# A decoder trunk on one core: high weights against both activation halves in one 512-column matmul

## The chip, the cores and the metric

One core of one Trainium2 chip runs the whole program. The metric is device time in microseconds (us). The core's engines are TensorE (PE; its loads of the standing operand are listed as PEld), VectorE (DVE), ScalarE (ACT), GpSimd (POOL) and SyncE (SP), which issues most DMA transfers. SBUF is the working memory; TensorE writes its results to PSUM, in tiles that VectorE and ScalarE read.

## The reference

Two layers of a decoder on 256 tokens of 2048 channels, in float32. A layer normalises x, multiplies it by one wide matrix, runs four branches on slices of the result, gates and projects each branch, adds the four, projects once more and adds to x.

```python
h = rms_norm(x, g_pre[l])
(s5_u, s5_z, ml_q, ml_k, ml_v, ml_o, ml_z, ml_i, ml_f,
 da_q, da_k, da_v, da_z, xa_q, xa_z, gate_pre) = split_cols(h @ w_in[l], IN_SPLITS)
y_s5 = s5_mixer(s5_u, ...) * silu(s5_z)        # diagonal state space, then a GLU: y * sigmoid(y @ w_glu + b)
y_ml = mlstm_mixer(ml_q, ml_k, ...) * silu(ml_z)   # ml_q, ml_k go through a 4-tap causal convolution first
y_da = diff_attention(da_q, da_k, da_v, ...) * silu(da_z)
y_xa = memory_attention(xa_q, rms_norm(mem, g_mem[l]), xa_w_kv[l]) * silu(xa_z)
merged = sum(sigmoid(gate_pre[b]) * (y_b @ w_branch[l, b]) for b in the four branches)
x = x + rms_norm(merged @ w_out[l], g_post[l])
```

Each 1024-wide slice (s5_u, ml_q and so on) and both halves of xa_w_kv (K and V) are matrix products of depth 2048.

## The kernel before

**Split operands.** Every weight matrix and every activation is held as two float32r tiles: a rounded high half (wh, hh) and the remainder as a low half (wl, hl). A product is three matmuls: high x high, high x low, low x high, added up in PSUM (`mm3`, L354 to L358). hh and hl hold the normalised x, mh and ml the normalised memory, both transposed: channels on the 128 partitions, 256 tokens along the row.

**Units.** All weights come as one stream of 944 units in a fixed order (`plan`, `stream`). A unit is 512 KB, 128 partitions x 1024 values: two depth blocks of 128 by 512 output columns. SP loads it into `raw` (4 buffers); ScalarE copies it to `wh` (L303), VectorE writes `raw - wh` to `wl` (L206). Each has LA + 1 = 4 buffers, and `ahead` issues loads and splits of up to LA = 3 units beyond the one in use.

**Two kinds of group.** `tok_group` keeps activations standing in TensorE and streams 512 weight columns: the result has tokens on the partitions. `chan_group` keeps a 128 x 128 block of weights standing and streams the 256 tokens: the result has channels on the partitions. A unit holds 8 such blocks, 24 matmuls of 256 columns in this form, 12 of 512 columns in the other. A group runs over the whole depth (8 units; 4 in the GLU and in the branch projections) and fills two accumulator tiles `acc` of 128 x 512; there are four. `chan_group` serves K of the memory attention, s5_u, ml_q, ml_k, xa_q, xa_z, s5_z and the GLU; everything else is `tok_group`.

**Other work.** Branches, norms and the emptying of accumulators are Python generators. After each unit `used` calls `bg_step`, which lets each live generator issue its next piece; `evac` puts the pieces that empty a group's accumulators on that list. Each engine runs what it was given in the order of issue, so this list sets where a piece stands between the splits. `u_evac` writes s5_u to DRAM for the S5 branch (`s5_gen`), `conv_gen` is the convolution, `phase` a gate and a branch projection; `t2` is a pool of six scratch tiles, `ps` are PSUM tiles for small products.

**Order of a layer.** V, K, s5_u, the differential attention's projections, ml_v, ml_o, ml_z, ml_q, ml_k, the phase of the differential attention, xa_q, xa_z, the mLSTM's phase, s5_z, the memory attention's phase, the GLU, the S5 phase, the output projection. In layer 0, by the profile, K runs from 58.7 to 108.7 us, s5_u to 154.8, ml_q and ml_k from 493.7 to 587.6, xa_q and xa_z from 733.5 to 832.4, s5_z from 982.9 to 1029.4.

Of the kernel before, what the change touches and what calls it, by code (L numbers as in the profile page):

```python
# [8 lines left out]
F32 = mybir.dt.float32  # L9
# [81 lines left out]

def in_groups():
    g = []
    for c0, n in ((S5U, 2), (DAQ, 2), (DAK, 2), (DAV, 2), (DAZ, 2), (MLV, 2), (MLO, 2), (MLZ, 2), (MLQ, 2),
                  (MLK, 2), (XAQ, 2), (XAZ, 2), (S5Z, 2), (GATE, 16)):
        for i in range(n):
            g.append(c0 + 512 * i)
    return g
# [3 lines left out]
GIDX = {c: i for i, c in enumerate(GROUPS)}  # L102


def layout(inp):
    a = {k: np.asarray(v) for k, v in inp.items()}
    out = {}
# [5 lines left out]
    out["w_kv"] = tile_w(a["xa_w_kv"])  # L113
# [40 lines left out]
INS = ("x", "mem", "w_in", "w_if", "w_kv", "w_br", "w_glu", "w_out", "cols", "s5_b", "s5_c", "lqk", "g_post", "consts")  # L154
# [3 lines left out]
def body(tc, x, mem, w_in, w_if, w_kv, w_br, w_glu, w_out, cols, s5_b, s5_c, lqk, g_post, consts, out,  # L158
# [4 lines left out]
    with ExitStack() as ctx:  # L163
# [81 lines left out]
        for l in range(depth):  # L245
            pl = {}
            for g in (2, 3, 0, 1):
                pl["kv", g] = add_units(w_kv[l, g], 8)

            def win(c0, l=l, pl=pl):  # L250
                pl["in", c0] = add_units(w_in[l, GIDX[c0]], 8)

            for c in (S5U, DAQ, DAK):
# [4 lines left out]
            for c in (MLV, MLO, MLZ, MLQ, MLK):  # L258
                win(c)
                win(c + 512)  # L260

            def phase(b, l=l, pl=pl):
# [5 lines left out]
            for c in (XAQ, XAZ):  # L268
                win(c)
                win(c + 512)  # L270
            phase(1)
            win(S5Z)
            win(S5Z + 512)
# [147 lines left out]


# [38 lines left out]
        def norm_T(src, cl, gname, dst_h, dst_l):  # L461
# [8 lines left out]
            yield from scaled_T(src, cl, gname, dst_h, dst_l)  # L470

        def scaled_T(src, cl, gname, dst_h, dst_l):

            s, _ = COLS[gname]
            held = {}

            def st_T(j):
                p = ps()
                for i in range(2):
                    for t in range(2):  # L480
                        d = 2 * j + i
                        tr(p[:, i * 256 + t * 128:i * 256 + t * 128 + 128], src[t][:, d * 128:d * 128 + 128])
                held[j] = p

            def st_h(j):
                for i in range(2):
                    d = 2 * j + i
                    act(dst_h[d // 8][:, d % 8], held[j][:, i * 256:i * 256 + 256], AF.Identity, scale=cl[:, s + d:s + d + 1])

            def st_l(j):  # L490
                for i in range(2):
                    d = 2 * j + i
                    stt(dst_l[d // 8][:, d % 8], held[j][:, i * 256:i * 256 + 256], cl[:, s + d:s + d + 1],
                        dst_h[d // 8][:, d % 8], M_, S_)

            yield from ticks(8, 1, [(0, st_T), (1, st_h), (1, st_l)])

        def bank(hs):
            return lambda kb: hs[kb // 8][:, kb % 8]
# [17 lines left out]
        def mem_T(l, cl):  # L517
# [670 lines left out]
        mt, mh, mlo, mgen = mem_T(0, cl)  # L1188
# [28 lines left out]
        for l in range(depth):  # L1217
            pl = plan[l]
            last = l == depth - 1
            hh = [bigr("hh"), bigr("hh")]  # L1220
            hlo = [bigr("hl"), bigr("hl")]
            mhb, mlb = bank(mh), bank(mlo)
            xg = norm_T(x_t, cl, "g_pre", hh, hlo)
# [4 lines left out]
            for g in range(2):  # L1228
                o = tok_group(pl["kv", 2 + g], 8, mhb, mlb)
                evac(*[lambda: None] * 5,  # L1230
# [5 lines left out]
            for g in range(2):  # L1236
                o = chan_group(pl["kv", g], 8, mhb, mlb)
                evac(lambda o=o, g=g: [tt(blk2(kT8[:, (2 * g + i) * 512:(2 * g + i) * 512 + 512]), blk2(o[i]),
                                          mrb.unsqueeze(1).to_broadcast([128, 2, 256]), M_) for i in range(2)],
                     lambda g=g, vm=vm, kT8=kT8: g == 1 and [  # L1240
                         nc.gpsimd.dma_start(out=kdr, in_=kT8),
                         nc.gpsimd.dma_start(out=vdr, in_=vm.rearrange("p t d -> p (t d)"))])
            bg_finish(ng)
            hb, lb = bank(hh), bank(hlo)
# [96 lines left out]
            def conv_gen(o, dst, off, g):  # L1341
                tmps = {}

# [3 lines left out]
                def src(m):  # L1347
                    return o[m // 2][:, (m % 2) * 256:(m % 2) * 256 + 256]

                def c_a(i):  # L1350
                    tmps[i] = t2.tile([128, 2, 256], F32, name="cv", tag="t2")
                    for k in range(2):
                        m = 2 * i + k
                        blk = off + 4 * g + m
                        act(tmps[i][:, k], src(m), AF.Identity, scale=wc(3, blk), bias=pcol(cl, "conv_b", blk))

                def c_b(*js):
                    def f(i):
                        for j in js:
                            for k in range(2):  # L1360
                                m = 2 * i + k
                                stt(tmps[i][:, k, 3 - j:256], src(m)[:, 0:253 + j], wc(j, off + 4 * g + m),
                                    tmps[i][:, k, 3 - j:256], M_, A_)
                    return f

                def c_c(i):
                    act(dst[:, 4 * g + 2 * i:4 * g + 2 * i + 2], tmps[i], AF.Silu)

                yield from ticks((0, 3), 1, [(0, c_a), (1, c_b(0, 1)), (2, c_b(2)), (3, c_c)])

            s5b["rate"] = 0.5
            for c0, dst, off in ((MLQ, cq, 0), (MLK, ck, 8)):
                for g in range(2):
                    o = chan_group(pl["in", c0 + 512 * g], 8, hb, lb)
                    bg_add(conv_gen(o, dst, off, g))
# [41 lines left out]
            for c0, dst, fn in ((XAQ, xq, AF.Copy), (XAZ, xz, AF.Silu)):  # L1417
                for g in range(2):
                    o = chan_group(pl["in", c0 + 512 * g], 8, hb, lb)
                    evac(lambda o=o, g=g, dst=dst, fn=fn: [act(dst[:, 4 * g + 2 * i:4 * g + 2 * i + 2], blk2(o[i]), fn) for i in range(2)])  # L1420
                    if c0 == XAZ and g == 0:
                        bg_finish(mlb_)
                        kT8 = big("kT2").rearrange("p (b t) -> p b t", b=8)
                        vm = big("vm2").rearrange("p (t d) -> p t d", t=2)
                        nc.sync.dma_start(out=kT8, in_=kdr)
                        nc.sync.dma_start(out=vm, in_=vdr)
# [6 lines left out]
            for g in range(2):  # L1433
                o = chan_group(pl["in", S5Z + 512 * g], 8, hb, lb)
                evac(lambda o=o, g=g: [act(sz[:, 4 * g + 2 * i:4 * g + 2 * i + 2], blk2(o[i]), AF.Silu) for i in range(2)])
# [90 lines left out]
            if not last:  # L1526
                cl_n = load_cols(l + 1)
                _, mh, mlo, mgen = mem_T(l + 1, cl_n)
# [91 lines left out]
```

## Time and profile before

| | |
|---|---|
| median of 3 runs | 2814.99 us (2811.59 to 2815.05) |
| the profiled execution | 2815.6 us, span 2813.8 us, mean granted TensorE clock 0.998 |
| TensorE | busy 2796.6 us (99%), 15604 matmuls |
| weight loads (PEld) | 2422.6 us (86%) |
| VectorE, ScalarE, GpSimd | 1999.0 us (71%), 1491.1 us (53%), 274.4 us (10%) |
| moved by DMA | 547.31 MB, mean 195 GB/s |
| chain that ended last | TensorE 96%, VectorE 2% |

Times count from the start of the span. A matmul's printed duration reaches to a modelled end and overlaps the next one; the distance from one start to the next is what a matmul takes of TensorE's time. In instruction names the tile written stands left of the arrow and the tiles read right of it; L is the line in the kernel.

### The profile page before, as it was taken

The numbers are of one execution on the slowest core, as the hardware profiler recorded it, in microseconds if no ns is written. First come the engines' busy times: TensorE is split into PE (matmuls) and PEld (weight loads), VectorE is DVE, ScalarE is ACT, GpSimd is POOL, SyncE is SP. The second block draws the span as 40 slices with busy tenths as digits, with TensorE's granted clock in tenths as the row PEclk, the third lists the DMA queues.
The fourth block names the chain that finished last, engine by engine and source line by source line (L and its number), as shares of the span: only waits on it lengthen the run. The fifth ranks groups of instructions, "written<-read, shape, count | busy, mean of one in ns | idle before, by whom it ended". The sixth has DMA issues, their size and how long they took to land.

```text
span 2813.8 us, 41302 instructions
## 1 busy us (share of the span) xinstructions
PE 2796.6 (99%) x15604; PEld 2422.6 (86%) x15604; DVE 1999.0 (71%) x3068; ACT 1491.1 (53%) x2116; POOL 274.4 (10%) x594
## 2 busy tenths in 40 slices
PE   9999999999999999999999999999999999999998
PEld 7988878988998898887889888789889988988887
DVE  6678787787778875555575787877887778665555
ACT  6445665465555544444454556655655555444443
POOL 1010122011110000000010102220112000000000
PEclk9999999999999999999999999999999999999999
DMA  7666556555565556556566665565555655566555
GB/s 253 222 207 200 171 163 196 189 181 189 174 223 178 180 188 209 189 188 225 211 221 212 208 195 175 165 196 184 190 183 175 224 166 189 191 209 203 189 189 183
DMA packets 164840, 547.31 MB, mean 195 GB/s; under 512 B 32192, under 2 KB 32576, under 8 KB 162336
## 3 DMA queue, kind: packets, MB, share of 16 engines
q1 hardware_dynamic: 141408, 512.60, 54.5%
q0 software_dynamic: 23232, 32.08, 4.1%
q8 instruction: 122, 2.00, 0.3%
q14 instruction: 78, 0.64, 0.1%
HBM read 531.80 MB, written 12.58 MB: 193 GB/s over the span
## 4 chain that ended last, share of the span: by engine, by line
PE 96%; DVE 2%; issue 0%; DMA 0%; POOL 0%; ACT 0%; SPq 0%; DVEq 0%; ACTq 0%; POOLq 0%
PE acc L356 30%; PE acc L357 30%; PE acc L358 30%; PE ps L361 3%; PE ps L364 2%; DVE wl L206 1%; PE yps L361 1%; PE ps L753 1%; DMA memt<-in_mem 0%; ACT wh L303 0%; POOL rz L442 0%; DVE s5b L206 0%; DVE s5a L206 0%; DVE o L214 0%; DVE das L214 0%
## 5 line engine op out<-in xcount | busy, mean ns | idle before, releaser
L206 DVE TENSOR_TENSOR wl<-raw,wh 128x1024 fp32r<-128x1024 f32 x942 | 1150.7, 1223 | 755.8 <-ACT wh L303 752.1
L303 ACT CAST wh<-raw 128x1024 fp32r<-128x1024 f32 x942 | 987.9, 1050 | 1212.8 <-PE acc L358 814.3
L356 PE MATMUL acc<-wh,hh 128*128 128x512 f32 x1920 | 759.1, 395 | 0.0
L357 PE MATMUL acc<-wl,hh 128*128 128x512 f32 x1920 | 748.5, 390 | 0.5 <-DVE wl L206 0.5
L358 PE MATMUL acc<-wh,hl 128*128 128x512 f32 x1920 | 748.4, 390 | 0.0
L356 PE MATMUL acc<-hh,wh 128*128 128x256 f32 x1536 | 435.7, 284 | 0.0
L357 PE MATMUL acc<-hl,wh 128*128 128x256 f32 x1536 | 434.6, 283 | 0.0
L358 PE MATMUL acc<-hh,wl 128*128 128x256 f32 x1536 | 434.6, 283 | 0.0
L356 PEld LDWEIGHTS acc<-wh,hh 128*128 128x128 f32 x1920 | 360.8, 188 | 78.5 <-issue 6.5
L358 PEld LDWEIGHTS acc<-wh,hl 128*128 128x128 f32 x1920 | 360.4, 188 | 76.8
L357 PEld LDWEIGHTS acc<-wl,hh 128*128 128x128 f32 x1920 | 361.0, 188 | 71.2 <-DVE wl L206 1.1
L356 PEld LDWEIGHTS acc<-hh,wh 128*128 128x128 f32 x1536 | 294.8, 192 | 1.9 <-issue 1.6
L357 PEld LDWEIGHTS acc<-hl,wh 128*128 128x128 f32 x1536 | 294.8, 192 | 0.2
L358 PEld LDWEIGHTS acc<-hh,wl 128*128 128x128 f32 x1536 | 294.8, 192 | 0.0
L356 PE MATMUL acc<-wh,th 128*128 128x512 f32 x248 | 98.2, 396 | 0.0
L357 PE MATMUL acc<-wl,th 128*128 128x512 f32 x248 | 97.2, 392 | 0.0
L358 PE MATMUL acc<-wh,tl 128*128 128x512 f32 x248 | 97.1, 392 | 0.0
L674 POOL DMA_DIRECT2D ur<-udr x64 | 44.4, 693 | 515.0 <-DVE bs L206 491.2
L203 ACT ACT_TABLE_LOAD x67 | 86.0, 1283 | 6.7 <-DMA cols<-in_cols 3.3
L434 POOL TENSOR_SCALAR rq<-rq 128x2 f32<-128x2 f32 x28 | 7.3, 261 | 789.4 <-DVE rz L430 789.4
L771 DVE TENSOR_TENSOR_SCAN s5b<-s5r,s5a 128x256 f32<-128x256 f32 x128 | 81.1, 674 | 0.1
L356 PE MATMUL acc<-mh,wh 128*128 128x256 f32 x256 | 73.8, 288 | 0.0
(314 smaller groups left out, 3742.6 us busy)
## 6 DMA issues: line engine op xcount, KB each, us to landing
raw<-in_w_in SPq DMA_DIRECT2D x672, 512.0 KB, 3.4
raw<-in_w_br SPq DMA_DIRECT2D x128, 512.0 KB, 3.4
raw<-in_w_kv SPq DMA_DIRECT2D x64, 512.0 KB, 3.4
raw<-in_w_out SPq DMA_DIRECT2D x64, 512.0 KB, 3.3
raw<-in_w_glu SPq DMA_DIRECT2D x16, 512.0 KB, 4.3
ur<-udr POOLq DMA_DIRECT2D x64, 96.0 KB, 5.0
br<-in_s_b POOLq DMA_DIRECT2D x64, 96.0 KB, 5.6
memt<-in_mem SPq DMA_DIRECT2D x16, 256.0 KB, 7.0
```

Source lines behind the costliest of these rows:

```text
L203: return S.activation(out=out, in_=in_, func=func, **kw)
L206: return V.tensor_tensor(out=out, in0=a, in1=b, op=op)
L303: S.copy(out=h, in_=r)
L356: nc.tensor.matmul(o, lhsT=ah, rhs=bh, start=start, stop=False, skip_group_check=True)
L357: nc.tensor.matmul(o, lhsT=ah, rhs=bl, start=False, stop=False, skip_group_check=True)
L358: nc.tensor.matmul(o, lhsT=al, rhs=bh, start=False, stop=stop, skip_group_check=True)
L361: nc.tensor.matmul(o, lhsT=lhsT, rhs=rhs, start=start, stop=stop, skip_group_check=True)
L364: nc.tensor.transpose(o, i, ident)
L434: E.tensor_scalar(out=m, in0=m, scalar1=-0.5, scalar2=None, op0=M_)
L674: nc.gpsimd.dma_start(out=ur, in_=udr[c // 4, rows].unsqueeze(0).to_broadcast([3, 32, 256]))
L753: nc.tensor.matmul(pb[:, ri], lhsT=e["bs"][:, ri], rhs=e["us"], start=ri == 0, stop=True, skip_group_check=True)
L771: V.tensor_tensor_scan(out=e["tb"][:, ri], data0=rb, data1=e["ta"][:, ri], initial=0.0, op0=M_, op1=A_)
```

## The change

The activations' halves are stored side by side: four tiles `hhl` (and `mhl` for the memory), each with four depth blocks, and for each block 256 columns of the high half followed by 256 of the low one. Outside the GLU, `chan_group` gives way to `chan_half`: a unit is now four depth blocks by 256 output columns (`tile_c`), a group is a quarter of a 1024-wide output and takes four units. In a unit eight matmuls of 512 columns come first (a block of `wh` against both halves of the activations), then eight of 256 (a block of `wl` against the high half). The sum of the high-half products and the low-weight products stands in the left 256 columns of an accumulator, the products with the low activations in the right 256. So emptying takes two pieces, issued one unit apart: `part_a` copies the left half (ScalarE), `part_b` adds the right half (VectorE). Scaling, SiLU and convolution then read the copy. Units in the stream keep their number, size and place.

```diff
+def tile_c(w):
+
+    l, k, n = w.shape
+    return np.ascontiguousarray(w.reshape(l, k // 512, 4, 128, n // 256, 256).transpose(0, 4, 1, 3, 2, 5))
...
+CHAN = (S5U, MLQ, MLK, XAQ, XAZ, S5Z)
...
-            for g in (2, 3, 0, 1):
-                pl["kv", g] = add_units(w_kv[l, g], 8)
+            for g in range(2):
+                pl["v", g] = add_units(w_v[l, g], 8)
+            for q in range(4):
+                pl["k", q] = add_units(w_k[l, q], 4)
...
+            def wch(c0, l=l, pl=pl):
+                for q in range(4):
+                    pl["ch", c0, q] = add_units(w_ch[l, 4 * CHAN.index(c0) + q], 4)
...
+        def chan_half(first, nu, cat):
+
+            o = [acc(), acc()]
+            for u in range(nu):
+                wh, wl = use(first + u)
+                for k in range(4):
+                    for m in range(2):
+                        nc.tensor.matmul(o[m], lhsT=wh[:, k, m * 128:m * 128 + 128],
+                                         rhs=cat(4 * u + k).rearrange("p a t -> p (a t)"),
+                                         start=u == 0 and k == 0, stop=False, skip_group_check=True)
+                for k in range(4):
+                    for m in range(2):
+                        nc.tensor.matmul(o[m][:, 0:256], lhsT=wl[:, k, m * 128:m * 128 + 128],
+                                         rhs=cat(4 * u + k)[:, 0], start=False,
+                                         stop=u == nu - 1 and k == 3, skip_group_check=True)
+                used()
+            return o
+
+        def part_a(out, o):
+
+            for m in range(2):
+                act(out[:, m], o[m][:, 0:256], AF.Copy)
+
+        def part_b(out, o):
+
+            for m in range(2):
+                tt(out[:, m], o[m][:, 256:512], out[:, m], A_)
+
+        def pairs(name):
+
+            return [b8.tile([128, 4, 2, 256], F32R, name=name, tag="b8") for _ in range(4)]
+
+        def cat_of(ts_):
+            return lambda kb: ts_[kb // 4][:, kb % 4]
+
+        def part_of(ts_, i):
+            return lambda kb: ts_[kb // 4][:, kb % 4, i]
...
-            h = [bigr("mh"), bigr("mh")]
-            lo = [bigr("ml"), bigr("ml")]
-            return mt, h, lo, scaled_T(mt, cl, "g_mem", h, lo)
+            m = pairs("mhl")
+            return mt, m, scaled_T(mt, cl, "g_mem", m)
...
-                evac(*[lambda: None] * 5,
+                o = tok_group(pl["v", g], 8, mhb, mlb)
+                evac(*[lambda: None] * (5 if g == 0 else 0),
...
-            for g in range(2):
-                o = chan_group(pl["kv", g], 8, mhb, mlb)
-                evac(lambda o=o, g=g: [tt(blk2(kT8[:, (2 * g + i) * 512:(2 * g + i) * 512 + 512]), blk2(o[i]),
...
+            def k_scale(q):
+                ks = blk2(kT8[:, q * 512:q * 512 + 512])
+                tt(ks, ks, mrb.unsqueeze(1).to_broadcast([128, 2, 256]), M_)
+
+            for q in range(4):
+                o = chan_half(pl["k", q], 4, mcat)
+                evac(lambda o=o, q=q: part_a(blk2(kT8[:, q * 512:q * 512 + 512]), o),
+                     lambda o=o, q=q: (part_b(blk2(kT8[:, q * 512:q * 512 + 512]), o), k_scale(q)),
...
-            def u_evac(o, g):
-                for i in range(2):
-                    ut = t2.tile([128, 2, 256], F32, name="ut", tag="t2")
-                    act(ut, blk2(o[i]), AF.Copy)
-                    b0 = 4 * g + 2 * i
-                    nc.gpsimd.dma_start(out=udr[b0:b0 + 2].rearrange("b p t -> p b t"), in_=ut)
-
-            for g in range(2):
-                o = chan_group(pl["in", S5U + 512 * g], 8, hb, lb)
-                evac(lambda o=o, g=g: u_evac(o, g))
+            hcat, hb, lb = cat_of(hc), part_of(hc, 0), part_of(hc, 1)
+
+
+            def u_evac(o, q):
+                ut = t2.tile([128, 2, 256], F32, name="ut", tag="t2")
+                part_a(ut, o)
+                yield
+                part_b(ut, o)
+                nc.gpsimd.dma_start(out=udr[2 * q:2 * q + 2].rearrange("b p t -> p b t"), in_=ut)
+                yield
+
+            for q in range(4):
+                o = chan_half(pl["ch", S5U, q], 4, hcat)
+                bg_add(u_evac(o, q))
...
+                sm_ = t2.tile([128, 2, 256], F32, name="cs", tag="t2")
+                part_a(sm_, o)
+                yield
+                part_b(sm_, o)
+                yield
+                tmp = t2.tile([128, 2, 256], F32, name="cv", tag="t2")
+                for m in range(2):
+                    blk = off + 2 * q + m
+                    act(tmp[:, m], sm_[:, m], AF.Identity, scale=wc(3, blk), bias=pcol(cl, "conv_b", blk))
+                yield
+                for js in ((0, 1), (2,)):
+                    for j in js:
+                        for m in range(2):
+                            stt(tmp[:, m, 3 - j:256], sm_[:, m, 0:253 + j], wc(j, off + 2 * q + m),
+                                tmp[:, m, 3 - j:256], M_, A_)
+                    yield
+                act(dst[:, 2 * q:2 * q + 2], tmp, AF.Silu)
+                yield
...
-            for c0, dst, fn in ((XAQ, xq, AF.Copy), (XAZ, xz, AF.Silu)):
-                for g in range(2):
-                    o = chan_group(pl["in", c0 + 512 * g], 8, hb, lb)
-                    evac(lambda o=o, g=g, dst=dst, fn=fn: [act(dst[:, 4 * g + 2 * i:4 * g + 2 * i + 2], blk2(o[i]), fn) for i in range(2)])
...
+            def silu(dst, q):
+                act(dst[:, 2 * q:2 * q + 2], dst[:, 2 * q:2 * q + 2], AF.Silu)
...
+                o = chan_half(pl["ch", XAZ, q], 4, hcat)
+                evac(lambda o=o, q=q: part_a(two(xz, q), o), lambda o=o, q=q: part_b(two(xz, q), o),
+                     lambda q=q: silu(xz, q))
...
+                o = chan_half(pl["ch", S5Z, q], 4, hcat)
+                evac(lambda o=o, q=q: part_a(two(sz, q), o), lambda o=o, q=q: part_b(two(sz, q), o),
+                     lambda q=q: silu(sz, q))
```

TensorE at the end of s5_u and the start of the next group (da_q), before:

```order
976 L356 MATMUL acc<-hh,wh 128x256
977 L357 MATMUL acc<-hl,wh 128x256
978 L358 MATMUL acc<-hh,wl 128x256
979 L356 MATMUL acc<-wh,hh 128x512
980 L357 MATMUL acc<-wl,hh 128x512
981 L358 MATMUL acc<-wh,hl 128x512
```

The first three rows are one block of weights; a unit is eight of these, one after another. At the same place of the changed kernel:

```order
273 L444 MATMUL acc<-hhl,wh 128x512 x8
274 L449 MATMUL acc<-hhl,wl 128x256 x8
275 L371 MATMUL acc<-wh,hhl 128x512
276 L372 MATMUL acc<-wl,hhl 128x512
277 L373 MATMUL acc<-wh,hhl 128x512
```

The first two rows are a whole unit, 16 matmuls where there were 24, and `wl` is first read after the eight wide ones; da_q keeps its form.

VectorE in the convolution of ml_q, layer 0 (`cv` is the convolution's sum, the numbers tell tiles of one name apart), before:

```order
L206 TENSOR_TENSOR wl_5320<-raw_5222,wh_5319 128x1024
L214 SCALAR_TENSOR_TENSOR cv_5282<-acc_4985,cols0_108,cv_5282 128x255 x2
L206 TENSOR_TENSOR wl_5352<-raw_5256,wh_5351 128x1024
L206 TENSOR_TENSOR wl_5389<-raw_5289,wh_5388 128x1024
L214 SCALAR_TENSOR_TENSOR cv_5382<-acc_4986,cols0_108,cv_5382 128x253 x2
L214 SCALAR_TENSOR_TENSOR cv_5382<-acc_4986,cols0_108,cv_5382 128x254 x2
```

The same engine and output in the changed kernel, where `cs` is the copy that `part_a` made:

```order
L222 SCALAR_TENSOR_TENSOR cv_4949<-cs_4890,cols0_108,cv_4949 128x255 x2
L214 TENSOR_TENSOR wl_5010<-raw_4931,wh_5009 128x1024
L214 TENSOR_TENSOR cs_5006<-acc_4866,cs_5006 128x256
L214 TENSOR_TENSOR cs_5006<-acc_4867,cs_5006 128x256
L214 TENSOR_TENSOR wl_5035<-raw_4956,wh_5034 128x1024
L214 TENSOR_TENSOR wl_5060<-raw_4986,wh_5059 128x1024
L222 SCALAR_TENSOR_TENSOR cv_5056<-cs_5006,cols0_108,cv_5056 128x253 x2
```

The two adds are new and stand between splits; the taps, which read the accumulators before, now read `cs`, so the accumulators are done with at the adds.

## Rows read from the trace of the kernel before

**Rows 1.** The page: engines' busy us (share) xinstructions; clock per slice.

```profile
PE 2796.6 (99%) x15604; PEld 2422.6 (86%) x15604; DVE 1999.0 (71%) x3068; ACT 1491.1 (53%) x2116; POOL 274.4 (10%) x594
...
PEclk9999999999999999999999999999999999999999
```

**Rows 2.** Waits of TensorE, whole span: us in total, times, longest.

```profile
PE ps L364 <- DMA memt<-in_mem: 3.4, 2, 2.1
PE ps L364 <- DVE ydal L214: 2.0, 2, 1.0
PE ps L361 <- DVE warm L1201: 1.3, 1, 1.3
PE acc L357 <- DVE wl L206: 0.8, 3, 0.3
```

**Rows 3.** Timeline, TensorE, S5 input projection of layer 0: start, duration, instruction.

```profile
108.72 0.28 PE L356 MATMUL acc<-hh,wh 128*128 128x256 f32 x1
108.84 0.28 PE L357 MATMUL acc<-hl,wh 128*128 128x256 f32 x1
...
154.69 0.28 PE L358 MATMUL acc<-hh,wl 128*128 128x256 f32 x1
154.81 0.40 PE L356 MATMUL acc<-wh,hh 128*128 128x512 f32 x1
155.04 0.40 PE L357 MATMUL acc<-wl,hh 128*128 128x512 f32 x1
```

**Rows 4.** Timeline, TensorE, one branch projection of 512 columns.

```profile
1085.42 0.39 PE L356 MATMUL acc<-wh,yxah 128*128 128x512 f32 x1
...
1096.07 0.39 PE L358 MATMUL acc<-wh,yxal 128*128 128x512 f32 x1
1096.30 0.39 PE L356 MATMUL acc<-wh,hh 128*128 128x512 f32 x1
```

**Rows 5.** Groups by line: xcount | busy us, mean ns | idle before.

```profile
L356 PE MATMUL acc<-hh,wh 128*128 128x256 f32 x1536 | 435.7, 284 | 0.0
L356 PE MATMUL acc<-mh,wh 128*128 128x256 f32 x256 | 73.8, 288 | 0.0
...
L356 PEld LDWEIGHTS acc<-hh,wh 128*128 128x128 f32 x1536 | 294.8, 192 | 1.9 <-issue 1.6
```

**Rows 6.** Windows: length, busy us of PE, PEld, DVE, ACT, POOL; PEclk, DMA share, GB/s.

```profile
58.70:108.70 50.00, 50.00 (x421) 49.96 (x421) 39.84 (x101) 25.63 (x38) 0.80 (x4) 1.00 0.54 180
108.72:154.81 46.09, 46.09 (x387) 46.09 (x386) 20.80 (x18) 18.26 (x19) 2.75 (x4) 1.00 0.70 240
493.70:587.60 93.90, 93.90 (x791) 93.14 (x790) 69.23 (x105) 48.70 (x65) 4.37 (x7) 1.00 0.58 189
733.50:832.40 98.90, 98.90 (x824) 97.83 (x824) 75.55 (x119) 51.98 (x72) 11.99 (x25) 1.00 0.62 210
982.90:1029.40 46.50, 46.50 (x389) 46.49 (x388) 36.10 (x51) 23.72 (x30) 1.31 (x2) 1.00 0.58 190
1085.42:1096.30 10.88, 10.88 (x50) 9.01 (x48) 4.90 (x4) 5.20 (x6) 0.00 (x0) 1.00 0.61 195
```

**Rows 7.** Groups by line on VectorE and ScalarE.

```profile
L206 DVE TENSOR_TENSOR wl<-raw,wh 128x1024 fp32r<-128x1024 f32 x942 | 1150.7, 1223 | 755.8 <-ACT wh L303 752.1 <-PE yps L361 0.8
L206 DVE TENSOR_TENSOR rb<-acc,cst 128x256 f32<-128x256 f32 x32 | 11.9, 415 | 0.0
...
L303 ACT CAST wh<-raw 128x1024 fp32r<-128x1024 f32 x942 | 987.9, 1050 | 1212.8 <-PE acc L358 814.3 <-PE acc L357 317.2 <-issue 38.4
L203 ACT ACTIVATE mh<-ps,cols 128x256 fp32r<-128x256 f32 x32 | 13.4, 472 | 11.2 <-PE ps L364 11.2
```

**Rows 8.** Waits of ScalarE, whole span.

```profile
ACT wh L303 <- PE acc L358: 814.3, 514, 5.1
```

More of the change, by code (lines that the diff above doesn't have):

```diff
@@ L112, in layout @@
     out["w_if"] = np.ascontiguousarray(w[:, :, MLI:MLI + 8].reshape(L, 16, 128, 8).transpose(0, 2, 1, 3))
-    out["w_kv"] = tile_w(a["xa_w_kv"])
+    out["w_ch"] = np.concatenate([tile_c(w[:, :, c:c + 1024]) for c in CHAN], axis=1)
+    out["w_k"] = tile_c(a["xa_w_kv"][:, :, :1024])
+    out["w_v"] = tile_w(a["xa_w_kv"][:, :, 1024:])
     out["w_br"] = tile_w(a["w_branch"].reshape(L * 4, 1024, D)).reshape(L, 4, 4, 4, 128, 2, 512)
@@ L151, in layout, with body @@
     return out
-INS = ("x", "mem", "w_in", "w_if", "w_kv", "w_br", "w_glu", "w_out", "cols", "s5_b", "s5_c", "lqk", "g_post", "consts")
+INS = ("x", "mem", "w_in", "w_ch", "w_if", "w_k", "w_v", "w_br", "w_glu", "w_out", "cols", "s5_b", "s5_c", "lqk", "g_post", "consts")
 LA = 3
-def body(tc, x, mem, w_in, w_if, w_kv, w_br, w_glu, w_out, cols, s5_b, s5_c, lqk, g_post, consts, out,
+def body(tc, x, mem, w_in, w_ch, w_if, w_k, w_v, w_br, w_glu, w_out, cols, s5_b, s5_c, lqk, g_post, consts, out,
          depth=L, taps=None):
@@ L257, in body @@
                 win(c)
-            for c in (MLV, MLO, MLZ, MLQ, MLK):
+            for c in (MLV, MLO, MLZ):
                 win(c)
                 win(c + 512)
+            wch(MLQ)
+            wch(MLK)
             def phase(b, l=l, pl=pl):
@@ L267, in body @@
             phase(2)
-            for c in (XAQ, XAZ):
-                win(c)
-                win(c + 512)
+            wch(XAQ)
+            wch(XAZ)
             phase(1)
-            win(S5Z)
-            win(S5Z + 512)
+            wch(S5Z)
             phase(3)
@@ L469, in norm_T, with scaled_T @@
             yield
-            yield from scaled_T(src, cl, gname, dst_h, dst_l)
-        def scaled_T(src, cl, gname, dst_h, dst_l):
+            yield from scaled_T(src, cl, gname, dst)
+        def scaled_T(src, cl, gname, dst):
             s, _ = COLS[gname]
+            dst_h, dst_l = part_of(dst, 0), part_of(dst, 1)
             held = {}
@@ L1187, in body @@
         nc.sync.dma_start(out=cl, in_=cols[0])
[L1188 removed]
+        mt, mc, mgen = mem_T(0, cl)
         x_t = [big("x"), big("x")]
@@ L1235, in body @@
             kT8 = big("kT")
-            for g in range(2):
-                o = chan_group(pl["kv", g], 8, mhb, mlb)
-                evac(lambda o=o, g=g: [tt(blk2(kT8[:, (2 * g + i) * 512:(2 * g + i) * 512 + 512]), blk2(o[i]),
-                                          mrb.unsqueeze(1).to_broadcast([128, 2, 256]), M_) for i in range(2)],
-                     lambda g=g, vm=vm, kT8=kT8: g == 1 and [
+            def k_scale(q):
[5 more added lines that the diff above has]
+                     lambda o=o, q=q: (part_b(blk2(kT8[:, q * 512:q * 512 + 512]), o), k_scale(q)),
+                     lambda q=q, vm=vm, kT8=kT8: q == 3 and [
                          nc.gpsimd.dma_start(out=kdr, in_=kT8),
@@ L1339, in body, with conv_gen @@
             ck = big("mlk").rearrange("p (b t) -> p b t", b=8)
-            def conv_gen(o, dst, off, g):
-                tmps = {}
+            def conv_gen(o, dst, off, q):
                 def wc(j, blk):
                     return pcol(cl, "conv_w", 16 * j + blk)
[L1347 to L1369, printed above, removed]
@@ L1371, in body @@
+                act(dst[:, 2 * q:2 * q + 2], tmp, AF.Silu)
+                yield
             s5b["rate"] = 0.5
             for c0, dst, off in ((MLQ, cq, 0), (MLK, ck, 8)):
-                for g in range(2):
-                    o = chan_group(pl["in", c0 + 512 * g], 8, hb, lb)
-                    bg_add(conv_gen(o, dst, off, g))
+                for q in range(4):
+                    o = chan_half(pl["ch", c0, q], 4, hcat)
+                    bg_add(conv_gen(o, dst, off, q))
             bg_finish(dab)
@@ L1416, in body, with two @@
             xz = big("xaz").rearrange("p (b t) -> p b t", b=8)
-            for c0, dst, fn in ((XAQ, xq, AF.Copy), (XAZ, xz, AF.Silu)):
-                for g in range(2):
-                    o = chan_group(pl["in", c0 + 512 * g], 8, hb, lb)
-                    evac(lambda o=o, g=g, dst=dst, fn=fn: [act(dst[:, 4 * g + 2 * i:4 * g + 2 * i + 2], blk2(o[i]), fn) for i in range(2)])
[L1421 to L1426, printed above, removed]
+            def two(dst, q):
+                return dst[:, 2 * q:2 * q + 2]
+            def silu(dst, q):
+                act(dst[:, 2 * q:2 * q + 2], dst[:, 2 * q:2 * q + 2], AF.Silu)
+            for q in range(4):
+                o = chan_half(pl["ch", XAQ, q], 4, hcat)
+                evac(lambda o=o, q=q: part_a(two(xq, q), o), lambda o=o, q=q: part_b(two(xq, q), o))
+            for q in range(4):
+                o = chan_half(pl["ch", XAZ, q], 4, hcat)
+                evac(lambda o=o, q=q: part_a(two(xz, q), o), lambda o=o, q=q: part_b(two(xz, q), o),
+                     lambda q=q: silu(xz, q))
+                if q == 1:
+                    bg_finish(mlb_)
+                    kT8 = big("kT2").rearrange("p (b t) -> p b t", b=8)
+                    vm = big("vm2").rearrange("p (t d) -> p t d", t=2)
+                    nc.sync.dma_start(out=kT8, in_=kdr)
+                    nc.sync.dma_start(out=vm, in_=vdr)
             yxa = (bigr("yxah"), bigr("yxal"))
@@ L1432, in body @@
             sz = big("s5z").rearrange("p (b t) -> p b t", b=8)
-            for g in range(2):
-                o = chan_group(pl["in", S5Z + 512 * g], 8, hb, lb)
-                evac(lambda o=o, g=g: [act(sz[:, 4 * g + 2 * i:4 * g + 2 * i + 2], blk2(o[i]), AF.Silu) for i in range(2)])
+            for q in range(4):
+                o = chan_half(pl["ch", S5Z, q], 4, hcat)
+                evac(lambda o=o, q=q: part_a(two(sz, q), o), lambda o=o, q=q: part_b(two(sz, q), o),
+                     lambda q=q: silu(sz, q))
             s5t = {}
```

27 lines of the change are left out of this document (11 added, 16 removed).

## The prediction

> **What bounds the kernel now.** I read the page's busy shares and its slices first: TensorE is busy 2796.6 of 2813.8 us at the full granted clock in every slice, VectorE 71%, ScalarE 53% [rows 1]. Then I read what TensorE waits for: four entries, 7.5 us in all, and the split of the weights (wl) holds 0.8 us of them [rows 2]. So time is set by how closely the matmuls follow one another, and a change counts if it alters the number of matmuls or the distance between their starts. A matmul's "busy" mean is no price here: 0.283 us is printed for one of 256 columns, yet the starts lie closer than that, because ends are modelled. I therefore take distances between starts.
>
> In the first projection of the S5 branch nothing is mixed in: the first of 384 matmuls of 256 columns starts at 108.72, the first of the next group at 154.81. That is 46.09 / 384 = 0.1200 us each [rows 3]. In a branch projection 48 matmuls of 512 columns take from 1085.42 to 1096.30: 10.88 / 48 = 0.2267 us each [rows 4]. The granted clock is 1.00, the 2.4 GHz level, in both stretches [rows 6]. The two distances differ by 0.1067 us for 256 columns, so 256 columns themselves cost 0.1067 us, and both sizes carry the same remainder: 0.1200 - 0.1067 = 0.0133 us, 0.2267 - 0.2133 = 0.0133 us. That remainder is paid once per matmul, whatever its width.
>
> **The change, part by part.**
> 1. The matmuls. Of the "weights stationary" form there are 1536 + 256 matmuls on each of three source lines outside the GLU [rows 5], so 1792 blocks of 128 x 128 weights with three matmuls each: 3 x 0.1200 = 0.3600 us. After the change a block has one of 512 columns (high weights times both halves of the activations) and one of 256 (low weights times the high half): 0.2267 + 0.1200 = 0.3467 us. The columns streamed per block stay 768; only one remainder is saved, 0.0134 us. Sum: 1792 x 0.0134 = **24.0 us**, all of it on TensorE, which sets the end.
>  The new 512-column form is not in this trace with the weights standing still; the nearest row is the 512-column stream above, also one 128 x 128 load and 512 streamed columns of the same type. Bounds: at the dear end it costs what two of 256 do (0.2400 us, gain nothing); at the cheap end its columns alone (0.2133 us, gain 1792 x 0.0267 = 47.8 us). I take 0.2267, because that stream is the same instruction in all but whose data stands still. The hand-over between widths costs nothing: from 256 to 512 the starts are 154.69, 154.81, 155.04 [rows 3].
> 2. Loads of weights. 1792 of them go. Each is listed at 192 ns [rows 5], so someone could book 1792 x 0.192 = 344 us. But they start as often as the matmuls, 0.12 us apart, and lie beside them; I book nothing beyond the remainder above.
>  The Trainium skill, "Perfetto Trace Analysis", "Identifying the Most-Contended Engine", holds the loads' busy share for a better measure of TensorE than matmul busy time, and by it the S5 stretch is load-bound (46.09 of 46.09 us, against 9.01 of 10.88 in the 512-column stretch [rows 6]). The remainder is the same 0.0133 us in both stretches, though only one is full of loads, so the trace doesn't bear that reading out; what it would give is the third rival below.
> 3. Order inside a unit. The eight wide matmuls need only the high weights, so the low half is first needed 8 x 0.2267 = 1.81 us into the unit, where it was needed 0.24 us in. The high half's buffer comes free 8 x 0.1200 = 0.96 us before the unit's end. ScalarE's high split waits mainly for TensorE to give buffers back (814.3 us in 514 waits on one line alone [rows 8]), so it runs at its limit ahead. Both moves only loosen that; worth nothing, since TensorE hardly waits for the split.
> 4. Leaving the accumulators. Each of 7 outputs x 4 quarters x 2 layers = 56 groups now needs two ScalarE copies and two VectorE adds of 128 x 256. Prices: 0.47 us (mh from PSUM) and 0.415 us (rb from acc) [rows 7]; 112 of each, so at most 52 us on ScalarE and 46 us on VectorE, spread over both layers. The scaling of K, four VectorE instructions of 128 x 512 a layer, is kept but reads the copy. In the busiest stretches VectorE goes from 39.84 to 39.84 + 8 x 0.415 = 43.2 us of 48.3 (K), from 75.55 to 82.2 of 95.5 (cross-attention), from 36.10 to 39.4 of 44.8 (S5's z), from 69.23 to 75.9 of 90.5 (convolution) [rows 6]; each stretch is shortened by 0.0134 us per block. That is 84 to 89%: hidden beside TensorE as long as the lead of about three units lasts. Without that cover the price would be the whole 46 us.
> 5. The deadline. A group is now four units, 4 x 8 x 0.3467 = 11.1 us, half of before, and a pair of accumulators is wanted again one group after it was filled. Behind the waiting matmul stands all of TensorE. The chain: the copies are issued after the next unit and stand behind one high split (0 + 1.05 + 0.94 = 2.0 us after the group's end); the adds stand behind the low split of the fifth unit on, whose high half needs the first unit's wide part done (1.81 us), and so start after the copies at about 2.0 + 1.05 + 1.22 = 4.3 us and end at 5.1 us, by the prices of [rows 7]. Six microseconds are left; other VectorE work in between is some 1 to 3 us a unit. I book nothing. Not booked at all: at worst every group waits, see the rivals.
> 6. Transfers. The weights keep their 512 KB units. The fullest stretch (240 GB/s, 0.70 of the queues [rows 6]) gets 4% denser. Nothing booked. The S5 input is written out one VectorE add later, and its last quarter is read long after the first.
>
> Sum: -24.0 us. The profiled execution took 2815.6 us with a span of 2813.8, 1.8 us outside it; 2815.6 - 24.0 = 2791.6. The median of the runs shown, 2814.99, is 0.6 us below that execution, so I predict 2791.0 us.
>
> **The rivals.**
> - Part of the gain is eaten by waits. For it: VectorE at 84 to 89% comes in bursts, and TensorE does already wait for wl and for ydal, a VectorE result, at a few places [rows 2]. Against: those total under 3 us, and the low half's deadline moves 1.57 us back. Some 10 us of waits, about 0.18 us per group, gives 2801 us.
> - Slower: the adds miss the accumulators' deadline. Place: the first wide matmul of every quarter from the third on. It decides from the point where copies and adds end over 11.1 us after the group. To lose more than the gain plus 5.6 us the 56 groups must wait 29.6 / 56 = 0.53 us each; if each is late by one unit, 56 x 2.77 = 155 us, 2946 us. Against it: the six microseconds above.
> - Loads set the beat of the 256-column stream. Then with two loads in place of three a block would be bound by its columns, 768 / 256 x 0.1067 = 0.320 us, gain 1792 x 0.040 = 72 us: 2743 us. Against: the equal remainder.
> - No gain. Either the remainder goes with the columns, which stay 768 per block, or a wide matmul with standing weights costs two narrow ones. Both give the time of before, 2815 us. Against: a remainder that goes with the columns would double from 256 to 512, and it doesn't; and the 512-column stream costs less than two narrow ones. (The Trainium skill, "TensorE: Matmul & The Clock Gate", "Back-to-back issue gap", gives N/2.4 + 2.5 ns per matmul when warm; by that the gain would be 1792 x 2.5 ns = 4.5 us and the time 2810.5 us, an estimate from that page. The trace shows 120 and 227 ns where it gives 109 and 216.)
>
> **How the numbers follow.** Forecast 0.80; part eaten 0.08; slower 0.04; loads 0.03; no gain 0.05. A difference under 0.2% (5.6 us) can't be told from none. Faster: 0.80 + 0.08 + 0.03 = 0.91; same 0.05; slower 0.04. The forecast's own spread is some 4 us each way (the three runs differ by 3.5 us). The range takes in that and most of the eaten case: 2784 to 2801 us, leaving out the other three cases and the end of the eaten one.
>
> **What would show it.** In the S5 stretch of the profile after: eight starts 0.227 us apart, eight 0.120 apart, 128 blocks in 44.4 us instead of 46.1. Step 4: VectorE's sum up by about 46 us and no wait of a wide matmul for cs, ut or kT. Step 5 is wrong if such waits appear at a quarter's first matmul. The forecast fails if wide starts are 0.24 us apart, or if TensorE's waits exceed 15 us.

## The result, and the profile after

The changed kernel takes 2793.64 us (median of 4, 2792.53 to 2796.72), the kernel before, run beside it, 2814.27 us: 20.6 us less, ratio 0.9931 with a 95% interval of 0.9916 to 0.9947. One execution of a later run, at a mean granted clock of 0.751, took 3447.73 us and is left out of that run's time below. The forecast was 2791.0 us, range 2784 to 2801. The profiled execution has a span of 2792.1 us, 21.7 us less than before.

The page's busy shares and clock after, to be laid beside [rows 1]:

```profile
PE 2773.9 (99%) x13812; PEld 2324.9 (83%) x13812; DVE 2035.4 (73%) x3180; ACT 1514.5 (54%) x2208; POOL 276.0 (10%) x594
...
PEclk9999999999999999999999999999999999999999
```

TensorE lost 1792 of 15604 matmuls and 22.7 us of busy time; VectorE and ScalarE gained 36 and 23 us. TensorE is still the bound. What it waits for after (us in total, times, longest), against [rows 2]:

```profile
PE ps L379 <- DMA memt<-in_mem: 3.2, 4, 1.4
PE ps L379 <- DVE ydal L222: 2.0, 2, 1.0
PE acc L372 <- DVE wl L214: 1.5, 4, 0.8
PE ps L376 <- DVE warm L1251: 1.3, 1, 1.3
PE acc L371 <- ACT wh L318: 0.6, 1, 0.6
```

No wide matmul (L444) waits for a copy or an add: the quarters' deadline is kept at all 56 places. The five stretches of layer 0 with standing weights, by window (length; busy us of PE, PEld, DVE, ACT, POOL; clock, DMA share, GB/s), K, s5_u, convolution, cross-attention, s5_z:

```profile
57.43:106.07 48.64, 48.64 (x294) 43.25 (x293) 42.31 (x108) 28.79 (x45) 1.12 (x6) 1.00 0.59 186
106.07:150.76 44.69, 44.69 (x258) 39.34 (x257) 22.97 (x25) 18.31 (x24) 3.49 (x5) 1.00 0.77 255
490.07:581.10 91.03, 91.03 (x534) 79.60 (x532) 74.26 (x122) 53.34 (x79) 4.38 (x7) 1.00 0.61 195
727.06:823.16 96.10, 96.10 (x568) 84.34 (x566) 80.68 (x134) 54.28 (x82) 11.97 (x25) 1.00 0.67 215
973.67:1018.82 45.15, 45.15 (x262) 39.80 (x260) 38.25 (x58) 26.92 (x38) 1.31 (x2) 1.00 0.60 197
```

From first matmul to first matmul of the next stretch (before by the same rule, forecast by 0.0134 us per block):

| us | K | s5_u | conv | cross | s5_z | sum |
|---|---|---|---|---|---|---|
| before | 49.97 | 46.08 | 93.81 | 98.85 | 46.55 | 335.26 |
| forecast | 48.25 | 44.37 | 90.38 | 95.42 | 44.83 | 323.25 |
| after | 48.63 | 44.69 | 91.03 | 96.10 | 45.15 | 325.60 |

Layer 0 gained 9.66 us, layer 1 by the same count 9.67: 19.3 us in place of 24.0. The other 2.4 us of the span's difference lie outside: first matmul of the weights 0.66 earlier, V 0.66 and the output stretch of layer 0 1.86 shorter, the stretches between s5_u and the convolution 0.6 longer in sum. They aren't the change's: the first experiment, which has none of its gain, shows the output stretch 2.60 us shorter too. In the profile before, TensorE waits there for a transfer (memt), and the granted clock is near its lower level (0.5 of full, 1.2 GHz) for the next 3.5 us:

```profile
1323.19 0.61 PE L364 MATMUL ps<-cst,memt 128*128 128x128 f32 x3 [2.12 <-DMA memt<-in_mem]
1323.50:1327.00 3.50, 3.50 (x12) 2.75 (x10) 1.75 (x3) 0.84 (x2) 0.00 (x0) 0.51 0.97 349
```

The first line is from the timeline, the second a window. The profile after has no such stretch. A slice of the page is 70 us long, too coarse to show it in [rows 1].

So each block saves 10.8 ns, not 13.4. Where the rest went stands in the timeline of TensorE (start, duration, instructions merged to runs):

```profile
120.03 2.00 PE L444 MATMUL acc<-hhl,wh 128*128 128x512 f32 x8
121.87 1.12 PE L449 MATMUL acc<-hhl,wl 128*128 128x256 f32 x8
122.83 0.86 PE L444 MATMUL acc<-hhl,wh 128*128 128x512 f32 x3
```

Eight wide starts take 121.87 - 120.03 = 1.84 us, where 8 x 0.2267 = 1.813 was forecast; eight narrow ones 0.96, as forecast or a little less. Read to the nanosecond, the wide starts of a unit in the s5_u stretch are 233, 236, 228, 232, 231 and then 227 ns apart, the narrow ones 113, 119 and then 120. So a return from narrow to wide costs 27 ns over five starts; a turn to narrow gives back 8. In 224 units 19 ns are 4.3 of the missing 4.7 us.

The kernel before has this too, in one of its few such places, and I had read only the first two rows of it [rows 3]. Further rows there:

```profile
155.28 0.39 PE L358 MATMUL acc<-wh,hl 128*128 128x512 f32 x1
155.50 0.40 PE L356 MATMUL acc<-wh,hh 128*128 128x512 f32 x1
155.74 0.39 PE L357 MATMUL acc<-wl,hh 128*128 128x512 f32 x1
155.97 0.39 PE L358 MATMUL acc<-wh,hl 128*128 128x512 f32 x1
```

From 154.81 to 155.97 are five starts and 1.16 us; five times 0.2267 are 1.133.

### The profile page after: what moved, and what is told of

Read it like the earlier page. It is cut to its first block, busy times and chain, and to the rows that moved or that the text cites. A ratio compares the mean times of both kernels' runs of the same rounds, so it can differ in the third digit from the quotient of the medians.

```text
span 2792.1 us, 38012 instructions
## 1 busy us (share of the span) xinstructions
PE 2773.9 (99%) x13812; PEld 2324.9 (83%) x13812; DVE 2035.4 (73%) x3180; ACT 1514.5 (54%) x2208; POOL 276.0 (10%) x594
## 4 chain that ended last, share of the span: by engine, by line
PE 97%; DVE 1%; DMA 0%; ACT 0%; issue 0%; SPq 0%; POOL 0%; DVEq 0%; ACTq 0%; POOLq 0%
PE acc L371 23%; PE acc L373 23%; PE acc L372 23%; PE acc L444 15%; PE acc L449 8%; PE ps L376 3%; PE ps L379 2%; DVE wl L214 1%; PE yps L376 1%; PE ps L803 1%; DMA memt<-in_mem 0%; ACT wh L318 0%; PE acc L1013 0%; PE acc L1011 0%; DVE o L222 0%
## 5 line engine op out<-in xcount | busy, mean ns | idle before, releaser
L371 PE MATMUL acc<-wh,hhl 128*128 128x512 f32 x1920 | 759.2, 395 | 0.0
L372 PE MATMUL acc<-wl,hhl 128*128 128x512 f32 x1920 | 748.7, 390 | 0.5 <-DVE wl L214 0.5
L373 PE MATMUL acc<-wh,hhl 128*128 128x512 f32 x1920 | 748.5, 390 | 0.0
L371 PEld LDWEIGHTS acc<-wh,hhl 128*128 128x128 f32 x1920 | 360.7, 188 | 78.4 <-issue 7.1
L373 PEld LDWEIGHTS acc<-wh,hhl 128*128 128x128 f32 x1920 | 360.4, 188 | 76.6
L372 PEld LDWEIGHTS acc<-wl,hhl 128*128 128x128 f32 x1920 | 361.0, 188 | 72.2 <-DVE wl L214 1.7
L444 PE MATMUL acc<-hhl,wh 128*128 128x512 f32 x1536 | 385.5, 393 | 0.0
L444 PEld LDWEIGHTS acc<-hhl,wh 128*128 128x128 f32 x1536 | 276.5, 189 | 51.4 <-ACT cs L211 0.8
L449 PEld LDWEIGHTS acc<-hhl,wl 128*128 128x128 f32 x1536 | 209.5, 190 | 15.0
L449 PE MATMUL acc<-hhl,wl 128*128 128x256 f32 x1536 | 214.1, 282 | 0.0
L444 PE MATMUL acc<-mhl,wh 128*128 128x512 f32 x256 | 65.5, 398 | 0.0
L372 PEld LDWEIGHTS acc<-wl,th 128*128 128x128 f32 x248 | 46.6, 188 | 9.4
```

The source lines that it names most:

```text
L371: nc.tensor.matmul(o, lhsT=ah, rhs=bh, start=start, stop=False, skip_group_check=True)
L372: nc.tensor.matmul(o, lhsT=ah, rhs=bl, start=False, stop=False, skip_group_check=True)
L373: nc.tensor.matmul(o, lhsT=al, rhs=bh, start=False, stop=stop, skip_group_check=True)
L444: nc.tensor.matmul(o[m], lhsT=wh[:, k, m * 128:m * 128 + 128], rhs=cat(4 * u + k).rearrange("p a t -> p (a t)"), start=u == 0 and k == 0, ...
L449: nc.tensor.matmul(o[m][:, 0:256], lhsT=wl[:, k, m * 128:m * 128 + 128], rhs=cat(4 * u + k)[:, 0], start=False, stop=u == nu - 1 and k == ...
```

## The experiments

All are the changed kernel with one edit; the edits are shortened, with `...` where code is left out (`wide` and `narrow` issue one matmul of each kind). The theory: the gain is the number of matmuls, less what the turns between widths cost. Rivals: the price is a unit's start, not a turn; the gain comes in part from the new order or the shorter groups; the emptying costs something.

**Two narrow matmuls for one wide.**

```diff
-nc.tensor.matmul(o[m], lhsT=wh[...], rhs=cat(4 * u + k).rearrange("p a t -> p (a t)"), ...)
+for i in range(2):
+    nc.tensor.matmul(o[m][:, i * 256:i * 256 + 256], lhsT=wh[...], rhs=cat(4 * u + k)[:, i], ...)
```

> The changed kernel with each 512-column matmul of the high weights issued as two of 256 columns (high activations, then low ones); layout, unit order, quarters, copies and adds stay as changed. Theory (the number of matmuls is all there is to the gain): 24 matmuls of 0.120 us a unit again, so the five kinds of stretch take what they took before (46.1 us in the S5 input projection, 128 blocks), 1792 x 0.0109 us = 19.5 us over the changed kernel: about 2813 us, like before. Rival (the later need of the low half, the earlier return of the high half's buffer or the shorter groups gave part of the gain, or the copies and adds cost something): under 2808 us, or over 2818 us.

Measured: 2812.82 us beside 2812.98 before, ratio 1.0001 (0.9992 to 1.0010). The s5_u stretch by window:

```profile
107.96:154.04 46.08, 46.08 (x386) 46.08 (x385) 22.96 (x25) 18.23 (x24) 3.48 (x5) 1.00 0.73 245
```

46.08 us as before, though VectorE has the adds (22.96 us for 20.80 [rows 6]) and the order is the new one. The other stretches have their lengths of before too, so all of the gain is the wide matmul; order, early return of the high half and quarters give nothing, copies and adds cost nothing.

**Wide and narrow in turn, one by one and two by two.**

```diff
-for k, m in km: wide(k, m)
-for k, m in km: narrow(k, m)
+for k, m in km:        # by twos: both m wide, then both m narrow
+    wide(k, m)
+    narrow(k, m)
```

> The changed kernel with wide and narrow matmuls taking turns within a unit (wide, narrow, wide, narrow), nothing else. Theory A1 (every return from narrow to wide costs 27 ns, less 8 ns given back at the turn to narrow, 19 ns net): eight returns a unit in place of one, 7 x 19 x 224 = 30 us more, about 2823 us; S5 input stretch 46.8 us. Theory A2 (the price belongs to the length of the narrow run and comes in steps; a single turn pays only the first step, 233 + 113 = 346 ns per block against 349): about 2788 us, S5 input stretch 44.3 us. Rival B (the price is paid at a unit's start, whatever the widths): 2793.6 us, unchanged, with the five slow starts still after each unit's first matmul.

> The changed kernel with two wide and two narrow matmuls in turn (four returns to wide in a unit in place of one). Theory (each return pays the first steps of the same series, 233 and 236 ns, the turn to narrow gives back 113 and 119): 701 ns for two blocks, S5 input stretch 44.9 us. Rival (the series is cut short by the next narrow run and the rest is never paid, so that short runs cost less): under 44.7 us. Other rival (19 ns net for every return): 16 x 4 x 19 ns over 44.38 us, 45.6 us.

Measured: one by one 2796.31 us, ratio 0.9943 (0.9928 to 0.9958); two by two a single execution of 2790.96 us. The s5_u stretch, first by ones, then by twos:

```profile
106.37:151.60 45.23, 45.23 (x258) 39.24 (x257) 22.96 (x25) 19.18 (x25) 3.48 (x5) 1.00 0.74 250
```

```profile
106.11:150.70 44.59, 44.59 (x259) 38.91 (x258) 22.96 (x25) 19.00 (x24) 3.48 (x5) 1.00 0.74 254
```

In s5_u, 128 returns to wide in place of 16 cost 0.54 us, and 64 in place of 16 cost nothing (44.69 to 44.59). Over all ten stretches one by one takes 3.4 us more than the change and two by two 1.1 us less, and the stretches don't agree: cross-attention took 96.01 us one by one, 96.10 in the change. Neither form of the first theory held, and by twos the rival did (under 44.7): by ones a wide start takes 237 and a narrow one 117 ns on average, 7 ns net for a return, by twos 233, 231, 113, 119, then 233, 236, 116, 112, about 3 ns net. So 19 ns net for a return only holds after a run of eight. That the next narrow run cuts the series short fits the runs of two; the 237 and 117 of the single ones don't follow from it, and no run shows why. The rival of the unit's start falls: slow starts follow the turns.

**Every second unit turned round.**

```diff
+for fn in ((wide, narrow) if u % 2 == 0 else (narrow, wide)):
+    for k, m in km:
+        fn(k, m)
```

> The changed kernel with every second unit turned round: wide then narrow, next unit narrow then wide, so that there is one return from narrow to wide per two units. Nothing else. Theory A (the return from narrow to wide costs 27 ns, the turn to narrow gives back 8): 112 turns each way are gone, 112 x 0.019 = 2.1 us less, about 2791.5 us, S5 input stretch 44.4 us with slow wide starts in every second unit only, in its middle. Rival B (paid at a unit's start): unchanged, S5 input stretch 44.7 us, slow starts at each unit's first matmuls.

> Every second unit turned round, on the same chip. In the first profile its ten stretches took 20.7 us less than before, 1.4 us less than those of the changed kernel. Theory A (a turn costs): 1 to 3 us under the changed kernel, ratio to before 0.992. Rival B: the same time as the changed kernel.

> The changed kernel itself, beside the version with every second unit turned round, on one chip. The ten stretches of the quarters took 19.3 us less than before in its profile: ratio to before 0.9931, about 19.5 us.

Measured: 2791.12 us, ratio to before 0.9923 (0.9908 to 0.9938). TensorE in the s5_u stretch (the view cuts the two narrow runs, each sixteen long):

```profile
108.68 1.48 PE L448 MATMUL acc<-hhl,wl 128*128 128x256 f32 x11
110.00 3.82 PE L443 MATMUL acc<-hhl,wh 128*128 128x512 f32 x16
113.66 1.48 PE L448 MATMUL acc<-hhl,wl 128*128 128x256 f32 x11
```

Sixteen wide ones take 113.66 - 110.00 = 3.66 us, 0.03 over 16 x 0.2267: one series of slow starts for sixteen, in place of two. The stretch is 44.53 us long (44.69 after, 8 returns less: 20 ns each), and the unit's boundary in the middle of the wide run has no slow start. All ten stretches together save 20.7 us over before, 1.3 more than the change. Run side by side on one chip, this version took 2791.41 us (median of five; 0.9923, 0.9910 to 0.9936) and the changed kernel 2792.28 us (0.9927, 0.9915 to 0.9939), and the stretches had the same lengths again. The order by the medians is as the stretches say, but the intervals overlap: that it beats the changed kernel is shown by the stretches, not by the times.

**Narrow matmuls with half the load, or with 384 columns.**

```diff
-nc.tensor.matmul(o[m][:, 0:256], lhsT=wl[:, k, m * 128:m * 128 + 128], rhs=cat(4 * u + k)[:, 0], ...)
+nc.tensor.matmul(o[m][0:64, 0:256], lhsT=wl[:, k, m * 128:m * 128 + 64], rhs=cat(4 * u + k)[:, 0], ...)
```

```diff
+nc.tensor.matmul(o[m][:, 0:384], lhsT=wl[:, k, m * 128:m * 128 + 128], rhs=<the first 384 of both halves>, ...)
```

> A probe of the cost of a turn: the changed kernel with the narrow matmuls loading 64 of their 128 weight columns (half of the low weights' products is left out). The columns streamed and the order of widths stay. Theory L (at 256 columns the load of the next 128 weights isn't quite covered, so a narrow run starts 120 instead of 113 ns apart and leaves the loads behind, which the next wide matmuls pay): narrow starts 113 ns apart, wide ones 227 from the first on, S5 input stretch 16 x (8 x 0.113 + 8 x 0.2267) = 43.5 us in place of 44.7, run about 2793.6 - 1792/128 x 1.2 = 2777 us. Theory W (any change of width costs, whatever is loaded): starts unchanged, 233, 236, 228, 232, 231 after each narrow run, 44.7 us, 2793.6 us.

> The same probe from the other side: the narrow matmuls stream 384 columns (128 columns of low weights times low activations are added), loads stay whole. Theory L: 160 ns of columns cover a load, so nothing is left behind: narrow starts 160 + 13 = 173 ns apart, wide ones 227 from the first on, S5 input stretch 16 x (8 x 0.1733 + 8 x 0.2267) = 51.2 us. Theory W: the wide starts after each narrow run are slow as before, 51.5 us.

Measured, one execution each: 2784.43 and 2898.61 us; s5_u stretch 44.05 and 52.27 us. TensorE with half loads:

```profile
119.22 2.00 PE L444 MATMUL acc<-hhl,wh 128*128 128x512 f32 x8
121.06 1.08 PE L449 MATMUL acc<-hhl,wl 128*64 128x256 f32 x8
121.97 0.63 PE L444 MATMUL acc<-hhl,wh 128*128 128x512 f32 x2
```

and with 384 columns:

```profile
125.46 1.58 PE L449 MATMUL acc<-hhl,wl 128*128 128x384 f32 x8
126.88 2.01 PE L444 MATMUL acc<-hhl,wh 128*128 128x512 f32 x8
128.73 1.58 PE L449 MATMUL acc<-hhl,wl 128*128 128x384 f32 x8
```

Theory L is half right. Half loads bring the narrow run from 0.96 to 121.97 - 121.06 = 0.91 us; its first two starts are 118 and 117 ns apart, the others 113. So 7 of the 120 ns go away with the edit. The edit halves the loaded columns and with them the partitions written; that the load and not the output saves the 7 ns is likely, but no run separates the two. The wide run stays at 1.84 us with half loads and grows to 1.85 with 384 columns, where the slow starts go through the whole run and the narrow ones take 1.42 us for the 1.39 expected. So the slow starts are not the loads' arrears; they follow any change of width tried. What in TensorE makes them is open.

**Emptying two units later.**

```diff
-evac(lambda: part_a(...), lambda: part_b(...), ...)
+evac(*[lambda: None] * 2, lambda: part_a(...), lambda: part_b(...), ...)     # conv_gen and u_evac: two more yields
```

> The changed kernel with copies and adds of every quarter issued two units later, the last place before the next group but one claims the accumulators. Theory (deadline 11.1 us after the group, chain now done at about 5.1 us): two units are 5.6 us, the chain ends at about 10.7 us, so TensorE just keeps up where VectorE has little else and waits up to some 1 us at a quarter's first matmul where it has more: 0 to 20 us over the changed kernel (2793 to 2813 us), the waits on cs, ut, kT, xaq, xaz or s5z. Rival (much more room than worked out, the deadline is no matter): under 1 us of such waits, 2793 us. Other rival (the chain was already near its limit): over 1 us at nearly each of 56 groups, 2850 us or more.

Measured: 2798.27 us, ratio 0.9948 (0.9931 to 0.9965), 4.6 us over the change. TensorE's waits:

```profile
PE ps L379 <- DMA memt<-in_mem: 3.0, 3, 2.4
PE ps L379 <- DVE ydal L222: 1.9, 2, 1.0
PE acc L444 <- ACT wh L318: 1.8, 2, 0.9
PE ps L376 <- DVE warm L1251: 1.3, 1, 1.3
PE acc L372 <- DVE wl L214: 0.8, 3, 0.3
PE acc L444 <- DVE kT L214: 0.7, 1, 0.7
PE acc L444 <- DVE cs L214: 0.3, 2, 0.2
```

Wide matmuls now wait for the adds of K (kT) and of the convolution (cs), and twice for a high split: five waits at a quarter's first matmul. For the last kind, once in each layer, two chains end close together. The one of layer 0, on TensorE, ScalarE and VectorE:

```profile
571.73 1.48 PE L444 MATMUL acc<-hhl,wh 128*128 128x512 f32 x5 [0.90 <-ACT wh L318]
570.14 0.63 ACT L211 ACTIVATE mlk<-cv 128x512 f32<-128x512 f32 x1 [1.97 <-DVE cv L222]
570.68 1.03 ACT L318 CAST wh<-raw 128x1024 fp32r<-128x1024 f32 x1
571.16 0.75 DVE L214 TENSOR_TENSOR cs<-acc,cs 128x256 f32<-128x256 f32 x2
```

The split stands behind a SiLU that waited 1.97 us for the delayed taps of the convolution, and the late adds that free the accumulators end only at 571.91. The convolution stretches grow by 1.7 us each, K of layer 0 by 1.05 and s5_z by 0.28, where no wait is listed. In sum that is 5.1 us for 2.8 us of listed waits, since a wait is counted from the modelled end of the matmul before. Two units, 5.6 us, are just about the room there was; the rivals (no matter, or near the limit already) fall.

**Emptying done twice.**

```diff
 act(out[:, m], o[m][:, 0:256], AF.Copy)
+act(out[:, m], o[m][:, 0:256], AF.Copy)
...
+tt(twice, o[m][:, 256:512], out[:, m], A_)
 tt(out[:, m], o[m][:, 256:512], out[:, m], A_)
```

> The changed kernel with each copy and each add of the emptying done twice (the second add's twin goes to a scratch tile), nothing else: 112 more ScalarE copies (about 52 us) and 112 more VectorE adds (about 46 us). Theory (this work lies beside TensorE): 2793.6 us, at most 2 us more, though VectorE rises to some 96% in the stretch of K. Rival (VectorE has no room left in K and the cross-attention stretch): over 5 us more, with waits of TensorE for wl or for the adds.

Measured: 2794.24 us, ratio 0.9933 (0.9916 to 0.9949); every one of the ten stretches has its length of the changed kernel to 0.01 us. K of layer 0, by window, VectorE 44.83 of 48.70 us:

```profile
57.40:106.10 48.70, 48.70 (x294) 43.28 (x293) 44.83 (x115) 31.17 (x52) 1.68 (x4) 1.00 0.56 177
```

The work is hidden, and twice as much would be.

## Why the prediction was right, and what was off

**Step 1** (matmuls): the count and the two prices were right, one term was mis-sized. The first experiment gives the whole gain to the wide matmul. The sum's 24.0 us were 19.3 in the stretches. The sentence that failed is "The hand-over between widths costs nothing": I read two starts behind one hand-over, and its series is five starts long. It costs 27 ns for a return and gives back 8 for a turn, 4.3 us in 224 units; the last 0.4 us are rounding of the 0.0134 and of the 19 ns. Wide matmuls with standing weights reach 227 ns from the sixth on, so 0.2267 was the right price inside a run.

**Step 2** (loads): booking nothing was right, the reason was not. I called the remainder the same for both widths and paid once per matmul. With half the load a narrow start is 113.3 ns inside a run, just half of a wide one's 226.7, so by these figures the time goes with the columns, and 256 of them cost 0.113 us, not 0.1067. The other 6.7 ns of a narrow start are the ones that went away with half the load. The saving of 13.3 ns per block is then twice these 6.7: two narrow matmuls of 120 ns against one wide of 226.7, whose start shows none of it. That 13 ns stood at both widths is a coincidence. It didn't move the forecast, which took distances read from rows, but the two rivals held unlikely because of the equal remainder were dismissed for a wrong reason. A remainder that goes with the columns (in "No gain") was near the truth for wide matmuls, and loads that set the beat of narrow ones (2743 us) for the rest; that rival failed in letting the loads spread over the block, since in the changed kernel's narrow runs the starts are still 120 ns apart.

The Trainium skill, "Perfetto Trace Analysis", "Identifying the Most-Contended Engine", holds the loads' busy share for a better measure of TensorE than matmul busy time. The half loads agree with it in direction: the s5_u stretch went from 44.69 to 44.05 us. But of the 1.2 us that Theory L forecast there, only 0.64 came.

**Step 3** (order): no gain, as said; the first experiment shows it.

**Step 4** (emptying): an add took 417 ns (415 forecast), a copy 0.38 us (0.47). The 112 adds print 46.7 us, as forecast, but VectorE's busy time rose by 36: neighbours overlap, and a pair of adds shows 0.75 us, not 0.83. In the busiest stretches too it rose by less than forecast (42.31 of 48.64 us in K, forecast 43.2). Hidden, and by the last experiment with room for as much again.

```profile
L214 DVE TENSOR_TENSOR cs<-acc,cs 128x256 f32<-128x256 f32 x32 | 12.0, 417 | 0.0
```

```profile
L211 ACT ACTIVATE cs<-acc 128x256 f32<-128x256 f32 x32 | 10.4, 377 | 5.1 <-PE acc L449 5.1
```

**Step 5** (deadline): right, in the chain too. In the changed kernel a quarter of s5_u ends where the next begins, at 117.24, and its accumulators are wanted again at 128.41:

```profile
117.24 1.09 PE L444 MATMUL acc<-hhl,wh 128*128 128x512 f32 x4
120.36 1.23 DVE L214 TENSOR_TENSOR wl<-raw,wh 128x1024 fp32r<-128x1024 f32 x1 [1.57 <-ACT wh L318]
121.51 0.75 DVE L214 TENSOR_TENSOR ut<-acc,ut 128x256 f32<-128x256 f32 x2
128.41 0.86 PE L444 MATMUL acc<-hhl,wh 128*128 128x512 f32 x3
```

The adds stand behind the low split and end at 122.26, 5.0 us after the quarter (5.1 forecast), with 6.1 us left; 5.6 us of delay bring the first five waits. Room differs by place: the first K quarter of layer 0 ends at 69.9 and its adds at 79.1, 9.2 us later. The rival that would have made the kernel slower was real as a mechanism and far away as a case.

**Step 6** (transfers): right; the fullest stretch went from 240 to 255 GB/s and TensorE waits for no weights in the quarters.

Of "part of the gain is eaten" the first half came true: part was eaten, but by the turns and not by waits.

## What to carry to other kernels

Where TensorE is 99% busy, price matmuls by the distance between starts: one matmul of 512 columns in place of two of 256 was worth 13 ns inside long runs and 11 with the turns. Read a hand-over over as many starts as it takes to settle, and try the order: against runs of eight, runs of sixteen (every second unit turned round) took back 1.3 us in the stretches and runs of two 1.1, and only single turns were dearer, by 3.4. When a group is cut in half, work out its emptying chain against the shorter deadline, and delay it on purpose to see how much room there is.

## What the runs showed of the hardware

At the 2.4 GHz level, a run of 256-column matmuls goes at 120 ns a start with 128 weight columns loaded for each, and at 113.3 ns with 64 loaded and 64 partitions written. A run of 512-column ones goes at 226.7 ns. After a run of 256-column ones the next wide starts were 233, 236, 228, 232, 231 and then 227 ns apart, the same in every unit of the s5_u stretch, and also in the kernel before. With 384 columns between, all eight wide starts were uneven (224 to 236 ns) and the matmuls of 384 took 173 to 185 ns. The slow starts after a turn were not expected, and their cause was not found.
